# An encoder layer on one core: output weights loaded into the query and key buffers, first feed-forward columns placed inside the output projection

## The chip, the cores and the metric

The kernel runs on one core of a Trainium2 chip. A core has five engines that run side by side, each working through its own list of instructions in order: PE (TensorE, matrix products), ACT (ScalarE), DVE (VectorE), POOL (GpSimd) and SP (SyncE, which here only issues DMA transfers). An instruction that has to wait holds up everything behind it on its engine. The metric is the device time of one execution in microseconds (us); lower is better.

## The reference

One encoder layer on x of 2048 tokens by 1024 channels, all float32. It normalises, projects, mixes by two head groups side by side (dilated attention and a gated MLP), projects the joined halves out, adds, and ends with a squared-ReLU feed-forward part of width 4096.

```python
def hybrid_layer(x, g_pre_mix, w_in, sgu_ln_g, sgu_ln_b, sgu_w, sgu_b, w_out, g_post_mix,
                 g_pre_ffn, w_ff1, w_ff2, g_post_ffn, rel_bias):
    h = rms_norm(x, g_pre_mix)
    z = h @ w_in
    q, k, v, zu, zv = jnp.split(...)
    attn = dilated_attention(q, k, v, rel_bias).reshape(B, S, D_ATTN)
    sgu = spatial_gating(jax.nn.gelu(zu), jax.nn.gelu(zv), sgu_ln_g, sgu_ln_b, sgu_w, sgu_b)
    mix = jnp.concatenate([attn, sgu], axis=-1) @ w_out
    x = x + rms_norm(mix, g_post_mix)
    h = rms_norm(x, g_pre_ffn)
    f = jnp.square(jax.nn.relu(h @ w_ff1)) @ w_ff2
    return x + rms_norm(f, g_post_ffn)
```

## The kernel before, in words

Every float32 product is made of three matmuls: each operand is split into a rounded high part and a remainder (`wh` and `wl`, `mh` and `ml`, `hh` and `hl`, `fh` and `fl`), ACT writing the high part and DVE the remainder, and `mm3` (lines 84 to 86) multiplies low by high, high by low, and high by high. A weight piece of 128 rows by 512 columns is loaded by `piece` into a raw buffer (tile `wraw`) and split into one of eight pairs in the pool `weights`.

The program has three stages.

- **Stage 1** projects x into queries, keys, values and the gated MLP's second half.
- **Stage 2** runs the attention, 8 heads of 12 groups, as a pipeline of 112 steps. The generator `gate` holds PE work that does not depend on attention: the gated MLP's first half, and then, per tile of 128 tokens, the half of the output projection that the gated MLP feeds (PSUM tile `f2`, shown as `f` in the trace), written to DRAM as `part`. `filler` runs pieces of it between the parts of a step, up to a share that `plan` computes; `PRE` and `POST` are the nanoseconds of it that are kept for before the first step and after the last. The order on PE and ACT in stage 2 is fixed as it is written (`in_order`); on the other engines, and in stage 3, a scheduler sets it. In the last tile of `gate`, before the change, `c.wo` is loaded: the eight pieces of `w_out` that belong to attention. They take the buffers of the eight pieces that this tile is using.
- **Stage 3** first does the attention half of the output projection, tile by tile, 16 tiles of 128 tokens. For a tile, `operand` loads the attention output (`fa`) and the reciprocal denominators (`fr`, one row spread over 64 partitions), multiplies them on POOL and splits the product; 24 matmuls into `mo` follow; DVE adds `part` (tile `r`). `post` normalises and adds x (tile `xt`), and writes the result to DRAM as `x1d`. For the first eight tiles, `prep` normalises again (in place, in `r`) and turns the tile by eight transposes (`tp`) into `hh` and `hl`, which the feed-forward part reads. Each of the two norms takes a pass of ACT (`jk`) and two small POOL instructions (`rs`, lines 90 and 91). Then, in two halves of 1024 tokens and eight groups of 512 hidden columns, `ff1` (192 matmuls into `f`) and `ff2` (192 into `g`) run.

Buffers in stage 3 before: three for `r`, two for `xt`, three each for `fa`, `fr`, `mh`, `ml`, five for `fh` and `fl`; six PSUM banks shared by `mo`, `f` and `g`. The core of the loop:

```python
            ahead, behind = 2, 1
            ...
                if i + ahead < 16:
                    ops.append(operand(i + ahead))
                if i + 1 < 16:
                    rx.append(rest(i + 1))
                (mh, ml), (r, xt) = ops.pop(0), rx.pop(0)
                ...
                if len(old) == behind:
                    prep(*old.pop(0))
```

## Time and profile before

| what | value |
|---|---|
| time, median of 3 runs | 2503.76 us (2500.02 to 2510.98) |
| profiled execution: its time | 2515.86 us |
| profiled execution: its span | 2514.0 us |
| busy shares of the span | PE 95%, weight loads 80%, DVE 42%, ACT 37%, POOL 19% |
| stage 2 (409 to 949 us), PE busy | 488.4 of 540 us |
| projection in stage 3 (949 to 1095.5 us), PE busy | 110.1 of 146.5 us |
| the rest of stage 3 (1095.5 us to the end), PE busy | 1403.2 of 1418.5 us |

The span is the time between the first and the last record of the profiled execution; 1.86 us of its time lie around it. Matmuls overlap in the trace (each is shown some 0.4 us long and one starts every 0.23 us), so PE's busy time is not its work: waits are read from the gaps, work from the distance of starts.

### The profile page before, as it was taken

To read this page: it belongs to the slowest core of one execution; us is meant where nothing else is said; L and a number is where in the kernel's file an instruction comes from. 1 tells how busy PE (TensorE), PEld (TensorE's weight loads), DVE (VectorE), ACT (ScalarE), POOL (GpSimd) and SP (SyncE) were. 2 spreads that over 40 slices of the span, in tenths; PEclk is the share of its full clock that TensorE was granted. 3 is DMA by queue.
4 is the path that set the end of the run, shared out by engine and by line. 5 is a ranking of instruction groups with operands and counts; after the bars stand their busy time and mean duration, and the time that the engine had idled before them with its cause. 6 is when DMAs were issued, how large, how long until landed. Compare 5 with 4: busy or idle time off the path is not lost.

```text
span 2514.0 us, 31489 instructions
## 1 busy us (share of the span) xinstructions
PE 2390.3 (95%) x11591; PEld 2000.0 (80%) x11591; DVE 1063.1 (42%) x2246; ACT 934.9 (37%) x2053; POOL 471.2 (19%) x521
## 2 busy tenths in 40 slices
PE   7999999988899996799999999999999999999998
PEld 6787888878788885678888888888788888888887
DVE  5433523566766644551322322333722333233226
ACT  4424322366766673433221221123533122212213
POOL 4103103533222222420100110011211001001101
PEclk9999999989999998899999999999999999999999
DMA  7646365878777567761111111111611121111113
GB/s 269 215 138 201 130 189 159 203 175 195 202 175 173 142 153 204 231 232 59 51 47 38 56 47 49 51 51 59 201 59 51 34 67 46 48 42 51 51 43 125
DMA packets 222077, 296.13 MB, mean 118 GB/s; under 512 B 37089, under 2 KB 128740, under 8 KB 218852
## 3 DMA queue, kind: packets, MB, share of 16 engines
q1 hardware_dynamic: 214724, 273.15, 37.4%
q10 hardware_dynamic: 4640, 16.79, 1.7%
q0 software_dynamic: 2560, 4.20, 1.2%
q8 instruction: 91, 1.49, 0.2%
q14 instruction: 62, 0.51, 0.1%
HBM read 216.04 MB, written 82.74 MB: 119 GB/s over the span
## 4 chain that ended last, share of the span: by engine, by line
PE 75%; DMA 12%; DVE 4%; ACT 3%; issue 1%; POOL 1%; SPq 1%; DVEq 0%; ACTq 0%; POOLq 0%
PE f L84 10%; PE f L85 10%; PE f L86 10%; PE g L86 8%; PE g L84 8%; PE g L85 8%; PE mm L84 4%; PE mm L86 4%; PE mm L85 4%; DMA v<-vd 2%; DMA r<-part 2%; PE t L588 2%; PE o L617 1%; PE o L616 1%; PE s L508 1%
## 5 line engine op out<-in xcount | busy, mean ns | idle before, releaser
L85 PE MATMUL f<-hh,wl 128*128 128x512 f32 x1024 | 399.4, 390 | 2.2 <-DVE wl L57 2.2
L86 PE MATMUL f<-hh,wh 128*128 128x512 f32 x1024 | 399.4, 390 | 0.0
L84 PE MATMUL g<-wl,fh 128*128 128x512 f32 x1024 | 399.4, 390 | 0.0
L84 PE MATMUL f<-hl,wh 128*128 128x512 f32 x1024 | 399.2, 390 | 0.0
L86 PE MATMUL g<-wh,fh 128*128 128x512 f32 x1024 | 398.9, 390 | 0.0
L85 PE MATMUL g<-wh,fl 128*128 128x512 f32 x1024 | 398.8, 390 | 0.0
L979 POOL TENSOR_TENSOR sq<-sq 128x512 f32<-128x512 f32 x128 | 131.9, 1051 | 1161.2 <-ACT sq L978 1161.2
L56 ACT ACTIVATE wh<-wraw,gain 128x512 fp32r<-128x512 f32 x200 | 143.3, 724 | 505.8 <-PE g L86 423.3
L57 DVE SCALAR_TENSOR_TENSOR wl<-wraw,gain,wh 128x512 fp32r<-128x512 f32 x200 | 158.0, 797 | 268.5 <-ACT wh L56 265.6
L60 DVE TENSOR_TENSOR fl<-sq,fh 128x512 fp32r<-128x512 f32 x128 | 99.3, 776 | 394.9 <-ACT fh L59 385.9
L85 PEld LDWEIGHTS f<-hh,wl 128*128 128x128 f32 x1024 | 192.6, 188 | 42.6 <-DVE wl L57 2.6
L84 PEld LDWEIGHTS f<-hl,wh 128*128 128x128 f32 x1024 | 192.7, 188 | 40.0
L86 PEld LDWEIGHTS f<-hh,wh 128*128 128x128 f32 x1024 | 192.6, 188 | 39.9
L86 PEld LDWEIGHTS g<-wh,fh 128*128 128x128 f32 x1024 | 192.3, 188 | 39.8
L85 PEld LDWEIGHTS g<-wh,fl 128*128 128x128 f32 x1024 | 192.3, 188 | 39.6
L84 PEld LDWEIGHTS g<-wl,fh 128*128 128x128 f32 x1024 | 192.3, 188 | 39.6
L1006 DVE TENSOR_TENSOR acc<-g,acc 128x512 f32<-128x512 f32 x192 | 127.2, 688 | 165.1 <-PE g L86 165.1
L978 ACT ACTIVATE sq<-f 128x512 f32<-128x512 f32 x128 | 74.8, 597 | 290.5 <-PE f L86 283.3
L577 ACT ACTIVATE p<-p,m 128x256 f32<-128x256 f32 (+2 forms) x384 | 173.8, 458 | 23.7 <-DVE m L549 23.7
L60 DVE TENSOR_TENSOR wl<-wraw,wh 128x512 fp32r<-128x512 f32 x144 | 100.5, 698 | 175.1 <-ACT wh L59 173.8
L59 ACT CAST wh<-wraw 128x512 fp32r<-128x512 f32 x144 | 89.5, 622 | 186.1 <-PE f L86 172.6
L525 DVE CUSTOM_DVE_ANT_0 p<-s,bias 128x256 f32<-128x256 f32 (+2 forms) x384 | 121.1, 356 | 44.2 <-PE s L509 30.5
(156 smaller groups left out, 4170.7 us busy)
## 6 DMA issues: line engine op xcount, KB each, us to landing
wraw<-in_w_ff_dram SPq DMA_DIRECT2D x256, 256.0 KB, 2.7
wraw<-in_w_in_dram SPq DMA_DIRECT2D x72, 256.0 KB, 3.0
xt<-in_x_dram SPq DMA_DIRECT2D x32, 512.0 KB, 5.6
v<-vd SPq DMA_DIRECT2D x40, 256.0 KB, 6.3
v<-vd SPq DMA_DIRECT2D x8, 1088.0 KB, 7.9
hd<-ht ACTq DMA_DIRECT2D x16, 512.0 KB, 5.1
vd<-vt SPq DMA_DIRECT2D x16, 512.0 KB, 3.1
qd<-e SPq DMA_DIRECT2D x32, 256.0 KB, 2.8
```

The source lines that it names most:

```text
L56: nc.scalar.activation(hi, src, AF.Copy, scale=scale)
L57: nc.vector.scalar_tensor_tensor(lo, src, scale, f32(hi), ALU.mult, ALU.subtract)
L59: nc.scalar.copy(hi, src)
L60: nc.vector.tensor_tensor(lo, src, f32(hi), ALU.subtract)
L84: nc.tensor.matmul(out, lhsT=lh, rhs=rl, start=start, stop=False)
L85: nc.tensor.matmul(out, lhsT=ll, rhs=rh, start=False, stop=False)
L86: nc.tensor.matmul(out, lhsT=lh, rhs=rh, start=False, stop=stop)
L525: nc.vector.tensor_tensor_reduce(po, so, bo, -1.0, 1e38, ALU.add, ALU.min, o.nm[:, br, cc:cc + 1])
L577: nc.scalar.activation(p[:, at + lo:at + hi], p[:, at + lo:at + hi], AF.Exp, bias=o.m[:, br, cc:cc + 1], scale=-1.0, accum_out=o.dn[:, br, ...
L978: nc.scalar.activation(sq, b, AF.Relu)
L979: nc.gpsimd.tensor_tensor(sq, sq, sq, ALU.mult)
L1006: nc.vector.tensor_tensor(av, b, av, ALU.add)
```

## The change

What it does, part by part:

- `c.wo` is no longer loaded in the last tile of `gate`. `attn_piece` loads one piece in each of the steps 96 to 103, after the last scores, into the buffers of queries and keys (`qk_tiles`), which a context of their own (`c.qctx`) now keeps open until the projection is done. ACT's cast and DVE's subtraction of each piece stand in those steps.
- `POST` goes from 4000 to 14000 ns.
- Stage 3 loads `fr` ahead of `fa`, two tiles ahead of the multiplication's tile (`load_attn`), with two buffers each in place of three; `operand` only multiplies and splits, one tile ahead. `part` is loaded two tiles ahead, with four `r` buffers in place of three; three `xt` buffers in place of two.
- The second norm (`normed`) writes into `xt`, no longer in place into `r`; a tile is turned two tiles after its projection, no longer one.
- The first eight `w_ff1` pieces (`ws0`) are loaded in iterations 1 to 4, no longer in the last. Of the first group's 192 `f` matmuls, 96 (`ff1_unit`, columns 0 to 255 of the group) are placed between the `mo` matmuls of tiles 6 to 12; the other 96 come after the loop. `load2(0)` is called before them.
- `fh` and `fl` get two buffers in each of two pools; `gpost` and `gmix` share one buffer; `y` and `xp` move to another pool.

```diff
@@ stage 1 and 2
-        c.qk = c.fctx.enter_context(tc.tile_pool(name="s2q", bufs=2, side="right"))
+        c.qk = c.qctx.enter_context(tc.tile_pool(name="s2q", bufs=2, side="right"))
...
+        c.wo = []
+
+        def attn_piece(k):
+
+            if k % 4 == 0:
+                c.spare = qk_tiles(c)
+            t = c.spare[k % 4 // 2][:, 1024 * (k % 2):1024 * (k % 2) + 1024]
+            raw = fload(nc, c, a["w_out"][0][(k % 4) * P:(k % 4 + 1) * P, (k // 4) * 512:(k // 4 + 1) * 512]
+                        .rearrange("p (k t) -> p k t", k=4))
+            split_sbuf(nc, raw.rearrange("p k t -> p (k t)"), t[:, 0:512], t[:, 512:])
+            c.wo.append((t[:, 0:512], t[:, 512:]))
...
-                        if i == 15:
-                            c.wo.append(out_piece(k * P, n))
...
-        PRE, POST = 8 * 1000.0, 4 * 1000.0
+        PRE, POST = 8 * 1000.0, 14 * 1000.0
...
+            if sa >= NH * NG and len(c.wo) < 8:
+                attn_piece(len(c.wo))
@@ stage 3
-        def normed(x1):
+        def normed(x1, out):
             rs = meansq(x1)
-            nc.scalar.activation(x1, x1, AF.Copy, scale=rs)
+            nc.scalar.activation(out, x1, AF.Copy, scale=rs)
...
+        def ff1_unit(h, ws, c0, es, fs, pool):
+
+            hh, hl = h
+            bs = [pm.tile([P, 512], F32, name=f"f{m}", tag="mm3") for m in range(2 * len(es))]
+            for kc in range(8):
+                wh, wl = ws[kc]
+                for m, b in enumerate(bs):
+                    k, e = divmod(m, len(es))
+                    cs = slice(c0 + k * P, c0 + (k + 1) * P)
+                    ts = slice(es[e] * 512, (es[e] + 1) * 512)
+                    mm3(nc, b, wh[:, cs], wl[:, cs], hh[:, kc, ts], hl[:, kc, ts], kc == 0, kc == 7)
+                yield
...
-            om = octx.enter_context(tc.tile_pool(name="s3m", bufs=3, side="right"))
-            orp = octx.enter_context(tc.tile_pool(name="s3r", bufs=3))
+            om = octx.enter_context(tc.tile_pool(name="s3m", bufs=2, side="right"))
+            orp = octx.enter_context(tc.tile_pool(name="s3r", bufs=4, side="right"))
...
+            parts, xs = [load_part(0), load_part(1)], [load_x(0)]
+            loads = [load_attn(0), load_attn(1)]
+            ops = [operand(*loads.pop(0))]
+            old, ws0, fs0, fs1 = [], [], [], []
+            early = {6: 3, 7: 3, 8: 2, 9: 1, 10: 3, 11: 3, 12: 3}
             for i in range(16):
...
+                (mh, ml), r, xt = ops.pop(0), parts.pop(0), xs.pop(0)
                 if i + 1 < 16:
-                    rx.append(rest(i + 1))
-                (mh, ml), (r, xt) = ops.pop(0), rx.pop(0)
+                    ops.append(operand(*loads.pop(0)))
+                if i + 2 < 16:
+                    loads.append(load_attn(i + 2))
+                if i in (6, 10):
+                    unit = ff1_unit(h, ws0, 0, (i // 10,), fs0, fpa)
                 for n in range(2):
...
                     nc.vector.tensor_tensor(r[:, ns], b, r[:, ns], ALU.add)
+                    for _ in range((early.get(i, 0) + 1 - n) // 2):
+                        next(unit, None)
+                if len(old) == 2 or i == 9:
+                    turned(*old.pop(0)[1:])
+                if i + 2 < 16:
+                    parts.append(load_part(i + 2))
+                if i + 1 < 16:
+                    xs.append(load_x(i + 1))
+                if 1 <= i < 5:
+                    ws0 += [piece(nc, c, w1[kc * P:(kc + 1) * P, 0:512], scale=c.gffn[:, kc:kc + 1])
+                            for kc in range(2 * i - 2, 2 * i)]
+                if 0 < i <= 8:
+                    normed(*old[-1][:2])
+                post(i, r, xt)
                 if i < 8:
-                    old.append((r, h[0], h[1], i))
-            for x in late:
-                post(*x)
-
+                    old.append((r, xt, h[0], h[1], i))
+        c.qctx.close()
+        v0 = load2(0)
+        fpb = ctx.enter_context(tc.tile_pool(name="s3g", bufs=2))
+        for _ in ff1_unit(h, ws0, 256, (0, 1), fs1, fpb):
+            pass
```

How the built programs differ at three places. First SP's list of transfers where the projection's first loads stand, in the program of before (`rd` holds the denominators, `wraw<-in_w_out` are `c.wo`'s pieces, `r` is `part`'s tile):

```order
L570 DMA rd<-d 128x16
L711 DMA part<-ot 128x512
L66 DMA wraw<-in_w_out_dram 128x512 x2
L895 DMA fr<-rd 64x4x128
L66 DMA wraw<-in_w_out_dram 128x512
L895 DMA fr<-rd 64x4x128
L905 DMA r<-part 128x1024
L895 DMA fr<-rd 64x4x128
```

The same place in the program of the change:

```order
L66 DMA wraw<-in_w_ff_dram 128x512 x2
L721 DMA part<-ot 128x512
L66 DMA wraw<-in_w_ff_dram 128x512 x3
L942 DMA r<-part 128x1024 x2
L927 DMA fr<-rd 64x4x128 x2
L928 DMA fa<-od 128x4x128
L927 DMA fr<-rd 64x4x128 x2
L928 DMA fa<-od 128x4x128
```

The `c.wo` pieces are gone from here; eleven loads of feed-forward weights stand between the last ones of `part<-ot`, the last three of them behind the very last, and the first `r`, `fr` and `fa` follow behind those.

Second POOL's list from the first products `fa` on, before. `rs_10033` is the first norm's factor of tile 0, `rs_10084` that of tile 1, `rs_10093` the second norm's of tile 0, the one that the transposes need:

```order
L898 TENSOR_TENSOR fa<-fa,fr 128x512 x4
L90 TENSOR_SCALAR rs_10033<-ms_10031 128x1
L91 TENSOR_TENSOR rs_10033<-rs_10033,mhalf 128x1
L898 TENSOR_TENSOR fa<-fa,fr 128x512
L90 TENSOR_SCALAR rs_10084<-ms_10082 128x1
L91 TENSOR_TENSOR rs_10084<-rs_10084,mhalf 128x1
L898 TENSOR_TENSOR fa<-fa,fr 128x512
L90 TENSOR_SCALAR rs_10093<-ms_10091 128x1
L91 TENSOR_TENSOR rs_10093<-rs_10093,mhalf 128x1
```

And with the change, where `rs_10015` and `rs_10078` are the two factors of tile 0 and `rs_10085` the first of tile 1:

```order
L935 TENSOR_TENSOR fa<-fa,fr 128x512 x4
L90 TENSOR_SCALAR rs_10015<-ms_10013 128x1
L91 TENSOR_TENSOR rs_10015<-rs_10015,mhalf 128x1
L935 TENSOR_TENSOR fa<-fa,fr 128x512
L90 TENSOR_SCALAR rs_10078<-ms_10076 128x1
L91 TENSOR_TENSOR rs_10078<-rs_10078,mhalf 128x1
L90 TENSOR_SCALAR rs_10085<-ms_10083 128x1
L91 TENSOR_TENSOR rs_10085<-rs_10085,mhalf 128x1
L935 TENSOR_TENSOR fa<-fa,fr 128x512
```

The second factor of tile 0 now stands behind five products, before it stood behind six.

Third PE's list in the first half of tile 6, with the change: `tp` turns tile 3, and the first moved `f` matmuls, which read `hh` and `hl` of tiles 0 to 3, stand two `mo` matmuls behind it. Before, only `mo` rows stood around the transposes.

```order
L84 MATMUL mo<-ks,mh 128x512
L876 MATMUL tp_10381<-ident,xt_10145 128x128 x4
L876 MATMUL tp_10388<-ident,xt_10145 128x128 x4
L85 MATMUL mo<-ks,ml 128x512
L86 MATMUL mo<-ks,mh 128x512
L84 MATMUL f_10439<-hl_9937,wh 128x512
L85 MATMUL f_10439<-hh_9936,wl 128x512
L86 MATMUL f_10439<-hh_9936,wh 128x512
L84 MATMUL f_10440<-hl_9937,wh 128x512
```

The first transposes stand behind 72 `mo` matmuls (three tiles) with the change and behind 76 before, and later ones follow every 24 to 32 in both. Between the last attention product `o` of stage 2 and the first `mo` stand 69 `f` matmuls with the change, 21 before.

## Rows read from the trace of the kernel before

**Rows 1.** Stretches: busy us (and instructions) of each engine, granted clock, DMA share, GB/s.

```profile
409.00:949.00 540.00, 488.42 (x3162) 433.45 (x3160) 332.35 (x1197) 336.85 (x1053) 187.13 (x187) 0.94 0.73 181
949.00:961.30 12.30, 0.15 (x1) 0.00 (x0) 3.57 (x8) 3.61 (x7) 2.07 (x2) 0.61 0.82 223
961.30:1095.50 134.20, 109.90 (x447) 87.50 (x448) 74.73 (x88) 53.08 (x86) 48.11 (x59) 0.88 0.77 230
1095.50:1143.10 47.60, 45.44 (x193) 37.14 (x192) 22.52 (x29) 21.59 (x34) 9.86 (x13) 0.96 0.46 156
...
1080.00:1090.00 10.00, 10.00 (x44) 8.03 (x44) 6.18 (x7) 1.15 (x2) 0.79 (x2) 1.00 0.94 342
1200.00:1700.00 500.00, 500.00 (x2207) 414.17 (x2206) 160.55 (x232) 117.92 (x188) 49.47 (x48) 1.00 0.16 49
```

**Rows 2.** PE's waits from 949 to 1143 us: total us, times, longest.

```profile
PE tp L870 <- ACT r L863: 24.2, 7, 9.7
PE mo L84 <- ACT mh L59: 12.2, 1, 12.2
PE f L85 <- DVE wl L57: 2.2, 1, 2.2
```

**Rows 3.** PE in order of time: start, us, operation, [idle before, releaser].

```profile
948.75 0.40 PE L86 MATMUL f<-wh,xh 128*128 128x512 f32 x1
961.31 0.79 PE L84 MATMUL mo<-wl,mh 128*128 128x512 f32 x1 [12.17 <-ACT mh L59]
...
965.19 0.49 PE L86 MATMUL mo<-wh,mh 128*128 128x512 f32 x1
...
970.20 0.40 PE L86 MATMUL mo<-wh,mh 128*128 128x512 f32 x1
...
980.04 0.40 PE L86 MATMUL mo<-wh,mh 128*128 128x512 f32 x1
...
1000.39 1.10 PE L870 MATMUL tp<-ident,r 128*128 128x128 f32 x8
1001.25 0.48 PE L86 MATMUL mo<-wh,mh 128*128 128x512 f32 x1
```

**Rows 4.** Other engines' waits in the projection's loop, 961.3 to 1095.5 us.

```profile
POOL fa L898 <- DMA fa<-od: 23.2, 5, 6.6
...
ACT r L863 <- DMA x1d<-r: 10.3, 4, 3.5
```

**Rows 5.** The chain that ended last, 936 to 1000 us: start, us, what.

```profile
980.58 6.84 DMA fr<-rd
```

**Rows 6.** Transfers issued from 949 to 1096 us: count, KB each, median us to landing.

```profile
DMA packets 23044, 33.84 MB, mean 230 GB/s; under 512 B 1744, under 2 KB 15824, under 8 KB 23036
...
fr<-rd SPq DMA_DIRECT2D x29, 128.0 KB, 10.3
fa<-od SPq DMA_DIRECT2D x13, 256.0 KB, 8.3
```

**Rows 7.** All engines in order of time, at the projection's first tile.

```profile
954.68 0.62 SPq L895 DMA_DIRECT2D fr<-rd  x1
...
956.71 0.33 SPq L905 DMA_DIRECT2D r<-part  x1
...
959.36 1.25 POOL L898 TENSOR_TENSOR fa<-fa,fr 128x512 f32<-128x512 f32 x1 [6.14 <-DMA fr<-rd]
...
961.69 0.58 ACT L710 COPY ot<-f 128x512 f32<-128x512 f32 x1
```

**Rows 8.** Costliest groups, the page's part 5: busy us, mean ns.

```profile
L56 ACT ACTIVATE wh<-wraw,gain 128x512 fp32r<-128x512 f32 x200 | 143.3, 724 | 505.8 <-PE g L86 423.3
L57 DVE SCALAR_TENSOR_TENSOR wl<-wraw,gain,wh 128x512 fp32r<-128x512 f32 x200 | 158.0, 797 | 268.5 <-ACT wh L56 265.6
```

**Rows 9.** Waits in stage 2, 409 to 949 us: total us, times, longest.

```profile
PE o L616 <- DMA v<-vd: 16.7, 14, 3.3
...
ACT wh L59 <- DMA wraw<-in_w_out_dram: 6.3, 3, 4.0
```

More of the change, by code (lines that the diff above doesn't have):

```diff
@@ L879, in stage3, with load2, load_attn @@
         h = new_h()
-        w1s = []
-        with ExitStack() as octx:
-            op = octx.enter_context(tc.tile_pool(name="s3o", bufs=1, side="right"))
-            om = octx.enter_context(tc.tile_pool(name="s3m", bufs=3, side="right"))
-            orp = octx.enter_context(tc.tile_pool(name="s3r", bufs=3))
-            gmix = bcast_row(nc, op, a["g_post_mix"][0:1], D, "gmix")
-            def operand(i):
+        fpa = ctx.enter_context(tc.tile_pool(name="s3f", bufs=2))
+        def ff1_unit(h, ws, c0, es, fs, pool):
[9 more added lines that the diff above has]
+                yield
+            for k in range(2):
+                if len(fs) == k:
+                    fs.append(tuple(pool.tile([P, 1024], F32R, name=x, tag=x) for x in ("fh", "fl")))
+                fh, fl = fs[k]
+                for e in range(len(es)):
+                    ts = slice(es[e] * 512, (es[e] + 1) * 512)
+                    sq = wk.tile([P, 512], F32, name="sq", tag="sq")
+                    nc.scalar.activation(sq, bs[k * len(es) + e], AF.Relu)
+                    nc.gpsimd.tensor_tensor(sq, sq, sq, ALU.mult)
+                    split_sbuf(nc, sq, fh[:, ts], fl[:, ts])
+        def load2(g):
+            return [[piece(nc, c, w2[(4 * g + k) * P:(4 * g + k + 1) * P, n * 512:(n + 1) * 512]) for k in range(4)]
+                    for n in range(2)]
+        with ExitStack() as octx:
+            om = octx.enter_context(tc.tile_pool(name="s3m", bufs=2, side="right"))
+            orp = octx.enter_context(tc.tile_pool(name="s3r", bufs=4, side="right"))
+            gmix = bcast_row(nc, cst, a["g_post_mix"][0:1], D, "gmix", "gain")
+            def load_attn(i):
                 sl = slice(i * P, (i + 1) * P)
@@ L1013, in done @@
                 def done(i, bs):
-                    x1 = wk.tile([P, D], F32, name="xf", tag="xt3")
+                    x1 = wk.tile([P, D], F32, name="xf", tag="xt3", bufs=3)
                     rows = slice(i * P, (i + 1) * P)
@@ L1019, in done @@
                     ms = sm.tile([P, 2], F32, name="ms4", tag="ms4")
-                    y = wk.tile([P, D], F32, name="y", tag="y", bufs=1)
+                    y = ap_.tile([P, D], F32, name="y", tag="y", bufs=1)
                     for n, b in enumerate(bs):
@@ L1046, in stage3 @@
                 for g in range(NG):
-                    v = load2(g)
-                    fs = ff1(h, ws)
+                    v, fs = (v0, fs0 + fs1) if half == g == 0 else (load2(g), ff1(h, ws))
                     last = g == NG - 1
```

78 lines of the change are left out of this document (22 added, 56 removed).

## The prediction

> **What bounds the kernel now.** I read the stretches first. From 1200 to 1700 us PE starts 2207 matmuls in 500 us without a gap, one every 0.2266 us at full clock [rows 1]: the feed-forward part is PE's own work, and nothing in the change makes it less. Stage 2 has PE busy 488.4 of 540 us [rows 1], its gaps scattered over many small waits, the largest kind 16.7 us in 14 pieces [rows 9]. The stretch between the two is different: from 949.0 (the last `f2` matmul starts at 948.75 [rows 3]) to the first `g` at 1143.1 us pass 12.3 + 134.2 + 47.6 = 194.1 us [rows 1].
>
> How much of that is work? `mo` starts come every 0.2343 us (42 steps from 970.20 to 980.04 [rows 3]), so 384 take 90.0. Eight transposes hold PE for 0.86 us (1000.39 to 1001.25 [rows 3]), 64 take 6.9. 192 `f` at 0.2266 take 43.5. Sum 140.4. PE's waits are 24.2 + 12.2 + 2.2 = 38.6 [rows 2]. The rest, 194.1 - 140.4 - 38.6 = 15.1 us, is the lower clock after waits: the granted clock is 0.88 in the loop and 0.96 behind it [rows 1]; after the first wait, eight steps take 3.88 us (961.31 to 965.19 [rows 3]) where 1.87 would do. So some 54 us in this stretch are not work, and they are all that the change can reach.
>
> What stands behind the waits: the 12.2 us at the start end with ACT's `mh` cast, behind POOL's product and the `fr` transfer [rows 2, 7]. The 24.2 us are PE standing in front of the transposes until ACT has written the second norm. Behind that stand POOL, which reaches the norm's factor only after products that wait for `fa` (23.2 us) [rows 4] and `fr` (once 6.84 us on the chain [rows 5]), and ACT itself, 10.3 us, because the norm is written in place and the `x1d` transfer must have read `r` first [rows 4].
>
> **The change part by part.**
>
> *The moved `f` matmuls.* 96 of 192 go between the `mo` of tiles 6 to 12: 96 x 0.2266 = 21.8 us of PE work. They add no work; they are worth something only as far as they fill waits. I count the work as 140.4 as before.
>
> *The waits for the transposes (24.2 us and their clock).* The transposes stand at nearly the same place in PE's list (behind 72 `mo`, before 76), so turning a tile "two later" is not by itself what helps. What helps is upstream. The norm goes to `xt`: the 10.3 us of waiting for `x1d` [rows 4] have no cause left. Tile 0's second factor stands behind five products on POOL, before behind six. `fr` and `fa` are issued ahead of the `xt` load that waited for tile 0's `post` on SP. I followed tile 0 by hand: the fifth product needs `fa`'s second buffer free, which tile 2's split gives once the first tile's `mo` are through; with some 5 us to land and 1.25 for the product, the norm is there 18 us after the first `mo`, and PE reaches the transposes after 3 x 24 x 0.2343 + 2.0 = 18.9. Now it is there after 29.7 (first `mo` at 961.31, transposes at 980.04 + 0.9 + the wait of 9.7 [rows 2, 3], about 991). So that one goes. But it is close, and two buffers in place of three for `fa` and `fr` make the next loads later: tile 5's `fa` stands on SP behind an `r` load that needs the first tile's norm, so I expect some 3 us at tile 1, 1 us each at tiles 3 to 5, and 2 us in front of the first moved `f`, which need tile 3's `hh` and `hl` two `mo` after its transposes. Together 8 us, clock included. The bounds are 0 and all that is lost now, 24.2 plus the 13.1 of clock that is not the start's.
>
> *The start (12.2 us).* `POST` leaves 48 more matmuls, 11 us, behind the last attention product, so denominators and attention outputs are written before `f2` ends. But the loads do not start then. In SP's list eleven `w_ff` loads stand before the first `r`, `fr` and `fa`. With four raw buffers, the eleventh needs the seventh weight piece split; its pair of buffers is one of the eight that `f2`'s last tile is using, so the seventh is freed by nearly the last matmul. From the end of `f2`: the `ot` copy 0.58 [rows 7], the fifth to seventh casts partly behind it, two whole ones of 0.72, then the subtraction 0.80 [rows 8]: 2.8, with the fifth's remainder 3.2. Then SP issues one raw load and two `r` at 0.33, two `fr` at 0.62 [rows 7] and `fa`: to 5.8. Before, 4.06 us passed from the end of the last `fr` issue to POOL's start (955.30 to 959.36 [rows 7]), then 1.95 to the first `mo` at 961.31. That gives 5.8 + 4.06 + 1.95 = 11.8 us. The wait stays, under another name: I take 12.0, with 2.0 of clock. Below, 4 us less if the weight chain runs ahead; above, 16 us, if `fr` lands as in the loop (10.3 us [rows 6]).
>
> *The wait at the first `f` (2.2 us)* goes: its weights are split before the loop.
>
> *DMA.* From 949 to 1096 us 33.84 MB move at 230 GB/s [rows 6]; the change takes some 2.5 MB of weights and `part` out and puts 1.2 MB of `fa` and `fr` in, about 33 MB. The loop as I sum it ends 12 + 2 + 90.0 + 6.9 + 21.8 + 8 = 140.7 us after `f2`, so 33 MB have 137 us: 240 GB/s. One stretch of ten us reached 342 at a share of 0.94 [rows 1]. The trace thus leaves room, and I charge nothing; at 230 it would be 7 us more. The Trainium skill says against it ("DMA: Bandwidth & Descriptors", section "Issuing engines are not separate DMA queues") that transfers issued from several engines run on the same 16 DMA engines and interleave, so that issuing earlier adds no capacity. By that rule alone, with the loop's mean rate taken as the capacity, the sum is 7 us worse; this trace's 342 GB/s says that the mean is not the capacity.
>
> *Stage 2.* PE's work stays; 10 us of filler leave the steps. Where PE waits for others anyway (a tenth of the time: 51.6 of 540 us [rows 1]) a step does not get shorter: about 1 us. The eight casts of `attn_piece` stand in ACT's fixed order and wait for their raw loads there; behind each stand the exponentials and the `th` casts that PE needs. The eight `w_out` casts already in stage 2 waited 6.3 us in 3 places, at most 4.0 [rows 9]; ACT is busy 336.9 of 540 us [rows 1] and so has slack: I take 1 us for PE. Together 2, bounds 0 and 8 x 4.0 = 32.
>
> *The rest.* The buffers of `fh` and `fl` fall from five to four, but `ff1` writes the next group's only after 96 matmuls (21.8 us), when the last group's readers on PE are done: 0, and without that cover one evacuation per group. `gpost` waits for `gmix`'s last use at the loop's end, seven groups of `ff1` and `ff2` before it is read: 0. `w_ff1`'s first pieces leave the end of the loop, which I have counted.
>
> **Sum.** 140.4 + 12.0 + 2.0 + 8 = 162.4 in place of 194.1: 31.7 less; stage 2 gives back 2: 29.7 less. The profiled execution took 2515.86, so 2486.2, which is 0.9882 of it; its time stands 12 us above the median of the runs, and 0.9882 of 2503.76 is 2474.
>
> **The rivals.**
> *DMA holds the loop* at its present 230 GB/s: 33 MB take 143.5 us from 3.5 us on, the loop ends 6 to 7 us later, 2481. For it: `fr` already lands after 10.3 us and `fa` after 8.3 [rows 6]. Against: the stretches at 342. The skill's rule above is this rival's.
> *The start is covered:* if the eleven `w_ff` loads do not hold SP, the filler hides the start, 12 + 2 us more gain: 2460. For it: everything that `fa` and `fr` need is written by then. Against: the order on SP.
> *The transposes' waits stay:* PE reaches them at the same place, and POOL's factor still stands behind products that wait for transfers. Then 24.2 + 13.1 in place of 8, gain below 1 us: 2503, no change. Half of it is 2489.
> *Slower:* the eight casts in stage 2 each hold ACT, and PE behind it. At 4.0 us each [rows 9] it is 32, and the gain is gone (2504); at 6 us each 48, 2520. It decides from about 4 us each. For it: the order on ACT is fixed and three raw buffers serve both the pieces and the filler. Against: `w_out` casts wait 6.3 us in all now.
>
> **How the numbers follow.** Forecast 0.57 (2466 to 2480 by itself), DMA 0.14, covered start 0.12, waits stay or half stay 0.11, stage 2 stalls 0.06. Two times are told apart here from about 0.5%, 12.5 us (below 2491 is faster). The forecast, DMA and the covered start are faster, and a part of the half-stayed waits: 0.85. No change: 0.09. Slower: 0.06. The range from 2457 (covered start, and a little less in the loop) to 2491 (half of the waits stay) leaves out both tails.
>
> **What would show it.** Right: the first `mo` some 12 us after the last `f2`, waiting for `mh` behind `fr` and SP behind the `wraw` loads; PE's waits for the transposes below 10 us; the loop some 141 us from `f2`'s end with 480 matmuls in it; 96 `f` (21.8 us) from there to the first `g`; stage 2 within 3 us of now. Wrong: `mo` starting right after `f2`; ACT waiting for `w_out` pieces in steps 96 to 103 by more than 10 us with PE gaps behind; a DMA share near 0.95 through the loop with PE waiting for `mh`.

## The result, and the profile after

The changed kernel takes 2538.33 us (median of 4 runs, 2537.27 to 2547.69), the kernel before beside it 2505.47 us: the ratio is 1.0139, 95% interval 1.0106 to 1.0173. It is 1.4% slower, where 1.2% faster was forecast. One of q13's five executions (3515.97 us) and one of q14's ten (3370.47 us) ran at a mean granted clock of 0.63 and 0.65, and no time or ratio below counts them. The profiled execution of the changed kernel took 2547.69 us, its span is 2545.9.

The stretches of the changed kernel, which answer to [rows 1] (same columns): stage 2, then from 949.0, 0.8 us after the end of `f2`, to the first `mo`, from there to the last `mo`, and from there to the first `g`.

```profile
409.00:948.20 539.20, 489.70 (x3156) 431.39 (x3155) 339.54 (x1205) 341.50 (x1061) 186.25 (x188) 0.94 0.73 185
949.00:969.10 20.10, 0.00 (x0) 0.00 (x0) 3.13 (x6) 3.34 (x6) 1.26 (x1) 0.59 0.71 203
969.10:1149.70 180.60, 133.03 (x543) 105.75 (x544) 78.61 (x97) 56.06 (x93) 41.94 (x65) 0.88 0.54 165
1149.70:1171.80 22.10, 22.10 (x99) 18.23 (x99) 8.56 (x11) 10.89 (x18) 3.92 (x8) 1.00 0.70 238
```

From the end of the last `f2` (948.2) to the first `g` (1171.8) pass 223.6 us, where 194.1 passed before and 162.4 were forecast. PE's waits in this stretch, which answer to [rows 2]:

```profile
PE mo L84 <- ACT mh L59: 24.6, 2, 20.8
PE tp L876 <- ACT xt L869: 18.6, 5, 7.0
PE f L84 <- DVE hl L76: 12.4, 2, 11.1
PE tp L876 <- DVE hl L76: 9.9, 2, 8.8
PE mo L85 <- DVE ml L60: 2.8, 2, 1.9
```

Their sum is 68.3 us; before it was 38.6. The work is 140.4 us as the prediction counts it, so 223.6 - 140.4 - 68.3 = 14.9 us are left for the lower clock, as 15.1 were before. The stretch is 29.5 us longer and the waits 29.7: all that was lost in it is waiting. Behind the first `g` the two kernels take the same time within 4 us (1374.1 and 1370.7 us to the end of the span).

In the loop, ACT no longer waits for `x1d` in front of the second norm (10.3 us before [rows 4]); it waits there for POOL's factor, 24.9 us in place of 18.2:

```profile
ACT xt L869 <- POOL rs L91: 24.9, 8, 6.0
```

So the waits for the transposes did not fall: 18.6 + 9.9 = 28.5 us, where 24.2 passed before.

The start, all engines in order of time (start, us, operation, wait before it): SP is at its `w_ff` loads until 954.3; the first `fr` is issued at 955.58, the first product starts at 967.15, the first `mo` at 969.12.

```profile
950.18 4.15 SPq L66 DMA_DIRECT2D wraw<-in_w_ff_dram  x3
954.74 0.80 SPq L942 DMA_DIRECT2D r<-part  x2
955.58 1.30 SPq L927 DMA_DIRECT2D fr<-rd  x2
956.92 0.60 SPq L928 DMA_DIRECT2D fa<-od  x1
...
967.15 1.26 POOL L935 TENSOR_TENSOR fa<-fa,fr 128x512 f32<-128x512 f32 x1 [24.50 <-DMA fr<-rd]
...
969.12 0.80 PE L84 MATMUL mo<-qs,mh 128*128 128x512 f32 x1 [20.76 <-ACT mh L59]
```

The loop around tiles 6 to 8, by the chain of work that ended last (start, us, what): one product, the next issue on SP, one transfer, the next product, and nothing beside it, a tile every 10 to 11 us.

```profile
1017.81 1.26 POOL fa L935
...
1019.38 0.29 SPq L927
...
1019.77 8.39 DMA fa<-od
...
1028.29 1.29 POOL fa L935
...
1029.89 0.29 SPq L927
...
1030.27 8.72 DMA fa<-od
...
1039.22 1.29 POOL fa L935
```

SP's own rows there tell why: `fr` of a later tile (line 927) stands ahead of `fa` of the next one (line 928), waits until a product has given its buffer free, and holds the `fa` load behind it, whose own buffer is free already (for the load at 1019.77 since 1013.1, when DVE had split tile 5).

```profile
1019.10 0.58 SPq L927 DMA_DIRECT2D fr<-rd  x1
1019.77 0.56 SPq L928 DMA_DIRECT2D fa<-od  x1
1020.38 0.67 SPq L927 DMA_DIRECT2D fr<-rd  x1
...
1029.60 0.58 SPq L927 DMA_DIRECT2D fr<-rd  x1
1030.27 1.29 SPq L928 DMA_DIRECT2D fa<-od  x1
1031.61 0.58 SPq L927 DMA_DIRECT2D fr<-rd  x1
```

In the built program the order on SP is fr(i+2), fa(i+1) from `fa` of tile 5 on. Before, `fa` of tile 8 was issued ahead of `part` of tile 4 (994.15 and 1002.37 us) and `fr` of tile 8 just behind it (from 1004.18). There, the attention loads ran about four tiles ahead of the rest.

That order is what holds the loads of tiles 6 to 10. Of the 47.5 us that PE waits in the loop, 27.6 come after 1062 us, where the products, but for the last, are 13.9 to 17.4 us apart, and there three things take turns on SP. `fa` of tiles 11 and 13 waits until DVE's split of the tile two before (`ml`) has given its buffer free:

```profile
1064.33 0.54 SPq L942 DMA_DIRECT2D r<-part  x1
1068.59 0.69 DVE L60 TENSOR_TENSOR ml<-fa,mh 128x512 fp32r<-128x512 f32 x1 [1.49 <-ACT mh L59]
1069.31 0.38 SPq L928 DMA_DIRECT2D fa<-od  x1
...
1092.36 1.03 SPq L947 DMA_DIRECT2D xt<-in_x_dram  x2
1094.88 0.68 DVE L60 TENSOR_TENSOR ml<-fa,mh 128x512 fp32r<-128x512 f32 x1
1095.59 1.66 SPq L928 DMA_DIRECT2D fa<-od  x1
```

`fa` of tiles 12 and 14 goes out behind `fr` of a later tile as above (`fr` at 1077.39 and 1108.46), and `fa` of tile 15 stands behind an `r` load that waits for `x1d` (until 1122.25). So the loop's loss has more than the one cause.

### The profile page after: what moved, and what is told of

Read it like the earlier page. It is cut to its first block, busy times and chain, and to the rows that moved or that the text cites. A ratio compares the mean times of both kernels' runs of the same rounds, so it can differ in the third digit from the quotient of the medians.

```text
span 2545.9 us, 31494 instructions
## 1 busy us (share of the span) xinstructions
PE 2393.3 (94%) x11591; PEld 1998.8 (79%) x11591; DVE 1061.1 (42%) x2246; ACT 933.7 (37%) x2053; POOL 457.5 (18%) x521
## 4 chain that ended last, share of the span: by engine, by line
PE 61%; DMA 10%; DVE 4%; ACT 3%; POOL 2%; issue 1%; SPq 1%; ACTq 0%; POOLq 0%; DVEq 0%
PE f L84 10%; PE f L85 10%; PE f L86 10%; PE g L86 8%; PE g L84 8%; PE g L85 8%; DMA fa<-od 3%; DMA v<-vd 2%; PE t L588 2%; PE o L617 1%; PE o L616 1%; PE s L508 1%; ACT p L577 1%; PE s L509 1%; POOL fa L935 1%
## 5 line engine op out<-in xcount | busy, mean ns | idle before, releaser
L84 PE MATMUL f<-hl,wh 128*128 128x512 f32 x1024 | 399.3, 390 | 12.4 <-DVE hl L76 12.4
L85 PEld LDWEIGHTS g<-wh,fl 128*128 128x128 f32 x1024 | 192.5, 188 | 39.8
L577 ACT ACTIVATE p<-p,m 128x256 f32<-128x256 f32 (+2 forms) x384 | 174.0, 459 | 18.9 <-DVE m L549 18.9
L60 DVE TENSOR_TENSOR wl<-wraw,wh 128x512 fp32r<-128x512 f32 x136 | 94.0, 691 | 167.9 <-ACT wh L59 166.6
```

The costliest lines, as they stand in the source:

```text
L60: nc.vector.tensor_tensor(lo, src, f32(hi), ALU.subtract)
L84: nc.tensor.matmul(out, lhsT=lh, rhs=rl, start=start, stop=False)
L85: nc.tensor.matmul(out, lhsT=ll, rhs=rh, start=False, stop=False)
L577: nc.scalar.activation(p[:, at + lo:at + hi], p[:, at + lo:at + hi], AF.Exp, bias=o.m[:, br, cc:cc + 1], scale=-1.0, accum_out=o.dn[:, br, ...
```

## The experiments

Each kernel was timed beside the kernel before. In the table, "start" is from the last `f2` to the first `mo`, "loop" from the first to the last `mo`, "behind" from there to the first `g`, and "stretch" their sum, all in us from the profiled execution. "Products" is the mean distance of POOL's products from the second to the last. The time of one kernel moves by up to 17 us from run to run (the kernel before: 2500.29 to 2517.43 in 23 runs), and in the profiles the last `f2` moves as far as that from kernel to kernel, so causes are read from the stretch. It comes from one profiled execution of each kernel, and how far it moves between executions is not known; the changed kernel and q9, whose lists on SP are the same from tile 5 on, agree in the loop to 0.1 us.

| kernel | start | loop | behind | stretch | products | time, us | ratio (95%) |
|---|---|---|---|---|---|---|---|
| before | 12.6 | 134.2 | 47.8 | 194.6 | 7.9 | | |
| changed | 21.2 | 180.6 | 22.0 | 223.8 | 11.3 | 2538.3 | 1.0139 (1.0106 to 1.0173) |
| q1 order on SP | 20.6 | 163.1 | 22.0 | 205.7 | 10.0 | 2532.7 | 1.0097 (1.0076 to 1.0118) |
| q2 no interleaving | 20.4 | 153.2 | 43.8 | 217.4 | 10.3 | 2543.2 | 1.0129 (1.0101 to 1.0158) |
| q3 before, two buffers | 11.9 | 149.3 | 47.4 | 208.6 | 9.8 | 2523.2 | 1.0059 (1.0036 to 1.0081) |
| q4 `w_ff` loads back | 17.2 | 182.6 | 22.0 | 221.8 | 11.5 | 2541.6 | 1.0138 (1.0117 to 1.0159) |
| q5 other memory | 8.4 | 188.8 | 22.0 | 219.2 | 11.8 | 2540.0 | 1.0126 (1.0111 to 1.0142) |
| q6 q5 and q1 | 8.7 | 171.9 | 22.0 | 202.6 | 10.5 | 2525.7 | 1.0063 (1.0040 to 1.0087) |
| q7 before, moved | 25.4 | 152.6 | 47.5 | 225.5 | 9.1 | 2527.0 | 1.0079 (1.0049 to 1.0108) |
| q8 three buffers | 20.1 | 166.4 | 22.0 | 208.5 | 9.7 | 2527.3 | 1.0086 (1.0058 to 1.0115) |
| q9 `r` one ahead | 19.5 | 180.6 | 22.0 | 222.1 | 11.3 | 2542.1 | 1.0142 (1.0123 to 1.0160) |
| q10 q6 and q9 | 8.9 | 169.0 | 22.0 | 200.0 | 10.3 | 2522.7 | 1.0064 (1.0045 to 1.0084) |
| q11 q10, three buffers | 9.7 | 169.2 | 22.0 | 201.0 | 10.0 | 2528.6 | 1.0089 (1.0072 to 1.0106) |
| q12 q10, half of `fr` | 7.8 | 165.6 | 22.0 | 195.4 | 10.0 | 2520.7 | 1.0053 (1.0034 to 1.0071) |
| q13 q10, further ahead | | | | | | 2529.8 | 1.0085 (1.0068 to 1.0102) |
| q14 q13, POST 4 | 19.4 | 165.3 | 22.0 | 206.7 | 10.0 | 2515.1 | 1.0026 (1.0015 to 1.0037) |
| q15 changed, POST 4 | 22.7 | 193.0 | 22.0 | 237.8 | 12.2 | 2552.1 | 1.0173 (1.0152 to 1.0195) |
| q16 before, POST 14 | 6.3 | 143.3 | 48.8 | 198.4 | 8.5 | 2520.6 | 1.0046 (1.0031 to 1.0062) |
| q17 before, norm apart | 13.0 | 125.8 | 56.0 | 194.9 | 8.0 | 2503.6 | 0.9990 (0.9973 to 1.0006) |
| q18 q17, four `r`, `xt` | 12.5 | 137.8 | 51.7 | 201.9 | 9.3 | 2513.9 | 1.0019 (1.0003 to 1.0035) |

The changed kernel's loop is 46.4 us longer than the one before, of which 21.8 are the moved `f`: 24.6 us were lost there, and 8.6 at the start.

### q1 and q8: the loads that stand behind each other on SP

q1 ties each attention load to the one written before it, so that SP issues them tile by tile; the tie sets an order and no wait.

```diff
+                for x in nc.cur_bb.bb.instructions[at:]:
+                    if "DMA" in type(x).__name__:
+                        if chain:
+                            tc.add_manual_dep(x, chain[-1].name, ..., reason="order")
+                        chain.append(x)
```

> The changed kernel, with SP's list of the attention loads made fr(i), fa(i), fr(i+1), fa(i+1); in the changed kernel fr(i+2) stands ahead of fa(i+1). Nothing else is asked for. Theory Q (order on SP: fa(i+1), whose buffer is free, stands behind fr(i+2), which waits for the product of tile i; load, product and next load run one after the other, 10.7 us per tile): POOL's products come every 8 to 9 us, the stretch from the first to the last mo falls from 180 to about 140 us, POOL's wait for fa from 74 us to below 30; about 2500 us. Theory D (the transfers themselves are at their limit): products still 10.7 us apart, 2538. Theory I (the interleaved f and the later turning hold ACT, DVE and POOL): within 5 us of 2538.

The loop falls by 17.5 us and the stretch by 18.1, so the order on SP is one cause. Theory Q had a loop of 140, and it is 163: a part of it. POOL's waits for `fa` did not fall below 30 us as it said, they are 92.5 (74.0 before the tie, with 32.2 for `fr` that are now gone). The times alone do not part the two kernels: their intervals overlap. Theory I, which expected no change, falls as the only cause.

q8 gives `fa` and `fr` the third buffer back, at the cost of one of `r`.

```diff
-            orp = octx.enter_context(tc.tile_pool(name="s3r", bufs=4, side="right"))
+            orp = octx.enter_context(tc.tile_pool(name="s3r", bufs=3, side="right"))
-                fa = om.tile([P, 4, P], F32, name="fa", tag="fa")
+                fa = om.tile([P, 4, P], F32, name="fa", tag="fa", bufs=3)
```

> The changed kernel, with three buffers for fa and fr in place of two, and three for r in place of four to make room; nothing else is edited. Theory Q: fr(i+2) has a free buffer when it comes to its turn on SP, fa(i+1) behind it goes at once, the products no longer come every 10.7 us: the loop falls from 180 to 160 us or less, the time to about 2520, or more where the missing r buffer makes SP wait. Theory D (the DMA engines are full): no change, 2538. The start stays at 20 to 21 us by either.

The loop falls by 14.2 us, to 166.4, short of the 160 of theory Q, with the start moved by 1.1 only. The time is 2527.3, so theory D, which expected 2538, falls. `mh` and `ml` keep their two buffers here.

### q3: two buffers in the kernel before

```diff
-            om = octx.enter_context(tc.tile_pool(name="s3m", bufs=3, side="right"))
+            om = octx.enter_context(tc.tile_pool(name="s3m", bufs=2, side="right"))
```

> The kernel before, with two buffers in place of three for fa, fr, mh and ml, and nothing else changed. Theory Q: the third buffer is what let the next loads go; without it load, product and split come closer to one chain, but fr and fa of one tile still stand side by side on SP: 2510 to 2530, PE's waits in the loop up by 5 to 25 us. Theory D and theory I: 2505, no change.

The loop grows by 15.1 us, the time by 0.6%. PE's waits, with the transposes' as they were (25.4 for 24.2) and a new one for `ml`:

```profile
PE tp L870 <- ACT r L863: 25.4, 8, 10.6
PE mo L84 <- ACT mh L59: 11.9, 2, 11.5
PE mo L85 <- DVE ml L60: 11.5, 3, 4.8
```

So with two buffers and nothing else of the change, the loop loses 15.1 us, where the changed kernel's loses 24.6. The prediction's 6 us for it (3 at tile 1, 1 each at tiles 3 to 5) were too few by 9. The edit takes the third buffer from `fa`, `fr`, `mh` and `ml` together; which of them costs what is not parted.

### q2: the interleaving

```diff
-            early = {6: 3, 7: 3, 8: 2, 9: 1, 10: 3, 11: 3, 12: 3}
+            early = {}
```

(with all 192 `f` behind the loop).

> The changed kernel with no f matmul between the mo: all 192 f stand behind the loop. Theory Q: the products stay some 10.7 us apart, so the loop is still 165 to 175 us, and the 96 f (21.8 us) that then stand behind it come on top: 2535 to 2560. Theory I: the loop falls by the 21.8 us of f and by the waits at the f as well, to about 135 us, and the time to about 2515. Theory D: as Q.

The loop is 27.4 us shorter, 21.8 of which are the `f` themselves, and 21.7 come back behind it. Theory Q had 165 to 175 for this loop and theory I 135; it is 153.2, between them. The stretch is 6.4 us shorter, and the time is not told apart from the changed kernel's. So the interleaving caused little of the loss, if any, and filled no waits that show: where `f` stands between the `mo`, PE waits in front of it instead (12.4 us for `hl` in the changed kernel), and with none there the transposes wait 31.7.

### q4, q5 and q7: the start

q4 puts the loads of the first `w_ff1` pieces behind the first attention loads.

> The changed kernel, with the loads of the first w_ff1 pieces put behind the first two fr and fa on SP (in the changed kernel eleven stand ahead of them). Theory H (the start is held by those loads, on SP and in the DMA queue): the first mo comes 9 to 12 us after the last f2, not 20.8, and the time falls by 8 to 12 us, to about 2528. If it were the writing of the denominators and attention outputs that ends last, the first mo stays at 20 us and the time at 2538. The loop behind it keeps its 10.7 us per tile in either case.

The start falls by 4.0 us only, and the time not at all, so theory H accounts for less than half of the 8.6 us that the start lost. In the built program lies another reason. Before, `fa`, `fr`, `mh` and `ml` are in the memory of queries and keys, which is free when the last scores are done: SP issues the first `fa` at 940.88, 8 us ahead of the last `f2`. The change puts the output weights there, and `fa`, `fr`, `mh` and `ml` fall on the addresses of `f2`'s operands `xh` and `xl` and of its result `ot`. q5 moves the first two tiles elsewhere, into the buffers that take `fh` and `fl` later:

```diff
-                fa = om.tile([P, 4, P], F32, name="fa", tag="fa")
-                fr = om.tile([P, 4, P], F32, name="fr", tag="fr")
+                if i < 2:
+                    two = fpa.tile([P, 8, P], F32, name="fafr", tag="fh")
+                    fa, fr = two[:, 0:4, :], two[:, 4:8, :]
```

> The changed kernel, with fa, fr, mh and ml of the first two tiles held in the buffers that later take fh and fl; nothing else is edited. Theory M (memory): with the output weights in the buffers of queries and keys, fa, fr, mh and ml lie where f2's operands and results lie, so their loads wait for the last f2 and for the last transfer of part; in the other place they are free when attention ends. By M the first two fr and fa are issued before f2 ends, the first mo starts 1 to 5 us after the last f2 in place of 21.2, and some 17 us go. Theory H (the w_ff loads on SP and in the DMA queue hold the start; held back by themselves they gave 4 us): the first mo comes at 17 to 21 us. The edit also moves SP's order: fr(i+2) stands ahead of fa(i+1) from tile 8 on, not from tile 5, so by theory Q the loop falls by some 6 to 10 us of the 17.5 that the full order gave. M and Q together: about 2513; H and Q: 2530.

The first `mo`, after an 8.0 us wait in place of 20.8:

```profile
957.47 0.79 PE L84 MATMUL mo<-qs,mhml 128*128 128x512 f32 x1 [8.02 <-ACT mhml L59]
```

The start falls by 12.8 us, to 8.4 (theory M had 1 to 5), and the first `fr` is issued at 945.22, ahead of the last `f2`. The edit moved the order on SP too: the `w_ff` loads now stand behind these first loads, from 952.98 on, and that alone gave 4.0 us in q4. If the two simply add, some 8.8 us are the memory's. But the loop takes 8.2 us back, and the time does not move by what can be told. q7 is the mirror, in the kernel before:

```diff
+            gap = pad.tile([P, 7168], F32, name="gap", tag="gap")
             om = octx.enter_context(tc.tile_pool(name="s3m", bufs=3, side="right"))
```

> The kernel before, with 28 KB of each partition left unused behind the gains, so that fa, fr, mh and ml lie where f2's operands lie; nothing else is edited. Theory M: fa of the first tiles, issued 6 to 8 us ahead of the last f2 in the kernel before, now waits for it; the first mo comes 18 to 21 us after the last f2, not 12.6, and the time is 6 to 10 us longer, 2512 to 2517. If the place of the buffers does not matter: 2505 and 12.6.

```profile
953.08 0.79 PE L84 MATMUL mo<-wl,mh 128*128 128x512 f32 x1 [25.02 <-ACT mh L59]
```

The start doubles, to 25.4 us, with no other line edited, and the loop grows by 18.4. The last `f2` came at 927.7 us, 21 earlier, so the time grew by 0.8% only; the last attention product stands 4.8 us ahead of it in both kernels, so the start did not grow by `f2`'s ending early. But the order on SP moved with the memory: the first `fa` now stands behind the first `r` loads and the last `part`. So place and order together cost the start, and no run moves the place alone.

### q6, q9, q10, q11: both together, and the loads of r

q6 is q5 with the tie of q1. q9 and q10 load `r` one tile ahead in place of two, in the changed kernel and in q6:

```diff
-            parts, xs = [load_part(0), load_part(1)], [load_x(0)]
+            parts, xs = [load_part(0)], [load_x(0)]
...
-                if i + 2 < 16:
-                    parts.append(load_part(i + 2))
+                if i + 1 < 16:
+                    parts.append(load_part(i + 1))
```

> The kernel of q5 with SP's attention loads in the order of q1 through the whole loop. M and Q: the start of q5 (1 to 5 us) and the loop of q1 (163 us from the first to the last mo, 180 in the changed kernel) add up: about 2503. If the two work on the same time (the loop waits for the same transfers, however early the first), the loop grows by what the start gives, and the time stays near 2520 to 2530.

> The changed kernel, with the load of r (rows of part) written one tile ahead in place of two; four buffers as before; nothing else is edited. Theory S (a load of r waits on SP for the x1d transfer of the tile whose buffer it takes, with the attention loads behind it; 51.5 us of such waits in the profile of q6): one ahead, the buffer is that of a tile earlier by one, long stored, and the loop falls by 5 to 20 us. Theory Q alone (fr(i+2) ahead of fa(i+1) is the lock; that order is left here): within 5 us of the changed kernel, 2538.

> The kernel of q6 with the loads of r one tile ahead in place of two. Theory S: SP's waits for x1d fall from 51.5 us to below 10, POOL's waits for fa from 47 us to below 30, the loop from 172 to 150 to 160 us, the time from 2526 to 2505 to 2515. Theory D (the transfers of fa, 8 to 12 us each, bound the loop, whatever stands ahead of them on SP): within 4 us of 2526.

q6 has both gains in the stretch, 202.6 us, 21.2 less than the changed kernel; against q1 its start falls by 11.9 us, of which the loop takes 8.8 back, and its time is the 2526 of the case in which the two work on the same time. q9 changes nothing (SP still waits 31.0 us for `x1d` in front of `r`), but it is no test of theory S in most of the loop: from tile 5 on the scheduler issued `r`, `fr` and `fa` in the order of the changed kernel. In q10 that wait falls from 57.6 to 33.6 us, not below 10, other loads wait in its place, and the loop falls by 2.9. Here too the order of q6 comes back, from `r` of tile 8 on. So theory S is not borne out, and not ruled out; the time, 2522.7, is what theory D named for this run. First q6, then q10, SP's waits from 945 to 1140:

```profile
SPq L960 <- DMA x1d<-r: 57.6, 11, 9.2
```

```profile
SPq L960 <- DMA x1d<-r: 33.6, 8, 6.4
SPq L935 <- DVE ml L60: 23.9, 6, 7.9
```

In q10 PE waits 39.8 us in all, as in the kernel before (38.6). With order, memory and `r` changed, the waits are back where they were before the change, and nothing is gained: the stretch is still 5.4 us longer than before. q11 adds the third buffers to q10, with three of `r`:

> The kernel of q10 with three buffers for fa and fr and three for r. Theory B (two buffers are too few for transfers of 9 us: the kernel before lost 14 us in this stretch with two): the loop falls by another 5 to 14 us, to about 2500, at or a little below the kernel before, since start and loop then have all that it has. Against it: with three buffers of r one ahead, r waits for x1d again, as in q6: 2515 to 2526.

It gained nothing (201.0 for 200.0); SP waits 49.1 us for `x1d` again, as the case against it said.

### q12: is it the DMA engines?

Half of the `fr` transfers from tile 3 on are left out; the tile takes the denominators of the tile before, so the products of these seven tiles are other numbers.

> The kernel of q10 with the transfers of fr left out for every other tile from tile 3 on, which takes the denominators of the tile before (so half of the products are other numbers). Theory D (the DMA engines' time, much of it in short packets of fr and fa, bounds the loop): 7 of 16 tiles lose 256 KB of such packets, at 4 to 5 us each: the loop falls by 15 to 30 us against q10. If it is the order and the buffers alone: below 8 us.

The loop falls by 3.4 us and the stretch by 4.6, below the 8 that were named for order and buffers alone. So the DMA engines' time is not what bounds q10's loop. In the changed kernel, where this was not tried, their share in the loop is 0.54, with 0.77 before.

### q13 to q16: looking further ahead, and POST

q13 lets loads and products run further ahead, with four sets of buffers up to tile 7; q14 is q13 with `POST` 4.

```diff
-                if i < 2:
+                if i < 8 and i % 4 < 2:
...
+                last = min(i + 2, 7) if i < 7 else min(i + 1, 15)
```

> The kernel of q10, with the attention loads three to four tiles ahead and the products two ahead up to tile 7 (one behind it): tiles 4 and 5 use the buffers of fh and fl again, as tiles 0 and 1 do, so four sets of buffers serve the first eight tiles. Theory L (lookahead): what makes the loop wait is that a load is issued only one product ahead, and lands 9 us later; four sets cover it, POOL's waits for fa fall from 73 to below 35 us, PE's waits in the loop from 31 to below 15, the stretch from the last f2 to the first g from 200 to 175 to 188, the time to 2498 to 2510. Theory D (the DMA engines' time): more loads at once share the same engines, each lands later, and the stretch stays at 195 to 202: 2518 to 2524.

> The kernel of q13 with POST 4 in place of 14. Theory P (with the start free, filler behind the last product covers the landing of the first denominators, and costs about as much ahead of it): first mo 12 to 15 us after the last f2 in place of about 9, last f2 4 to 8 us earlier, time within 5 us of q13. If the moved filler costs stage 2 more than it covers: 5 to 10 us below q13.

Of q13 only the time is used: 2530, outside what either theory named, so theory L is not borne out, and its waits are not known. q14 is the best of this row of kernels, 15 us below q13, more than either case had, and 0.3% above the kernel before. Its start is 19.4 us, not 12 to 15, since its first loads wait for the last attention outputs (SP issues `fr` at 946.80).

`POST` alone, in the changed kernel and in the kernel before:

```diff
-        PRE, POST = 8 * 1000.0, 14 * 1000.0
+        PRE, POST = 8 * 1000.0, 4 * 1000.0
```

> The changed kernel with POST 4 in place of 14, nothing else. Theory M (the first attention loads wait for the last f2 because of the memory they lie in): the filler behind the last product covers nothing, the first mo stays 20 to 22 us after the last f2, the last f2 comes 3 to 8 us earlier, and the time falls by that: 2530 to 2535. If the filler did cover the landing of the denominators: 2540 to 2548.

> The kernel before with POST 14 in place of 4, nothing else. Here the first fa lie in the buffers of queries and keys, free in time. Theory P: the first mo comes 4 to 8 us after the last f2 in place of 12.6, the last f2 3 to 5 us later, and the time falls by 0 to 5 us: 2502 to 2507. If the moved filler costs stage 2 more: 2510 to 2515.

Both times lie above all that was expected. In q15 the `w_ff` loads that stood ahead of the start move into the loop between the attention loads, ACT waits 19.2 us for them (4.0 in the changed kernel), and the loop grows by 12.4. In q16 the start falls from 12.6 to 6.3 us, as theory P said, and the loop takes 9.1 back. What `POST` costs stage 2 shows over all profiles: with 14, the last `f2` starts at 949.6 us in the mean of 12 kernels (943.1 to 958.3), with 4 at 943.6 in the mean of 6 (939.8 to 948.8; q7 not counted). The two ranges overlap, so the 6 us between the means are an estimate.

### q17 and q18: the norm by itself

The kernel before with the second norm written to `xt` (three buffers, in memory that lay unused), and then with four buffers of `r` and `xt`.

```diff
-            nc.scalar.activation(x1, x1, AF.Copy, scale=rs)
+            nc.scalar.activation(out, x1, AF.Copy, scale=rs)
```

> The kernel before, with the second norm written to xt in place of over r, and three buffers for xt (in memory that lay unused in the loop); nothing else is edited. If the norm over r is what holds ACT (10.3 us in front of the norm, and the transposes 24.2 us behind it): ACT's wait for x1d is gone, PE's waits for the transposes fall to 10 to 18 us, and the time by 4 to 12 us, to 2496 to 2504. If POOL's factor, which stands behind the products and their transfers, is what comes last: ACT waits for POOL in place of x1d, the transposes keep 20 to 25 us, and the time is within 4 us of 2508.

> The kernel of q17 with four buffers for r and xt. Theory S (r's loads wait on SP for x1d, 14.9 us in the kernel before, and hold the attention loads behind them): another 3 to 8 us less than q17. If the lead of the attention loads is enough here: within 3 us of q17.

q17's loop is 8.4 us shorter, and the wait for `x1d` in front of the norm is gone. In its place ACT waits 19.0 us for POOL's factor, and the transposes' waits fall from 24.2 to 18.9, so both cases had a part. But its first `f` are reached before their weights are split, and 8.2 us come back behind the loop; the time is the same. PE's waits in q17:

```profile
PE tp L870 <- ACT xt L863: 18.9, 5, 6.9
PE mo L84 <- ACT mh L59: 12.6, 1, 12.6
PE f L85 <- DVE wl L57: 7.5, 1, 7.5
PE f L84 <- ACT wh L56: 2.5, 1, 2.5
```

q18 lost the loop's gain again, against both of its cases. q17 with the early `w_ff1` pieces of the change, which would be there before the last two rows, was not tried.

## Why the prediction was wrong, step by step

The stretch was forecast at 162.4 us and took 223.6. The error of 61.2 us is 8.9 at the start, 51.9 in the loop and 0.4 behind it.

- **What bounds the kernel:** right. Of the 31.9 us by which the spans differ, 29.5 lie in the stretch that the prediction chose, and these are all PE's waits.
- **The loop's waits (forecast 8 us, clock included): the step that failed.** It said that the norm's wait for `x1d` has "no cause left", and that two buffers in place of three cost "some 3 us at tile 1, 1 us each at tiles 3 to 5". The first half is right: ACT no longer waits for `x1d`, and q17 gives 8.4 us in the loop for it. The second half followed SP's list by hand as far as tile 5, and just there the order turns: from then on fr(i+2) stands ahead of fa(i+1). The measured waits in the loop are 47.5 us; in front of the first moved `f`, priced at 2, they are 12.4. Of the 24.6 us that the loop lost, the order is worth 17.5 (q1) and two buffers by themselves 15.1 (q3); these overlap, as a third buffer for `fa` and `fr` gives back 14.2 (q8) and not the sum. What was priced at the first tiles is paid through the whole loop.
- **The waits for the transposes, expected below 10 us, measured 28.5:** they are the largest part of the 47.5. The rival by which they stay (0.11) had the reason, POOL's factor behind products that wait for transfers: ACT waits 24.9 us for it. It did not have the products coming 11.3 us apart in place of 7.9.
- **The start (forecast 11.8, measured 20.9):** the mechanism on SP was right, `w_ff` loads first and then `r`, `fr`, `fa`. The term that was mis-sized is the landing: 4.06 us were taken from the row of before [rows 7], 10.3 passed (956.88 to 967.15), and the issue came 2.9 us later than forecast. In the row of before `fa` had been loaded long since and only `fr` was under way; here `r`, `fr` and `fa` of two tiles go at once (that this is why they land later is argued, no run shows it). That the buffers had moved into `f2`'s memory was not seen. No attention load was issued before `f2` ended, as they were before the change and again in q5, so the covered start, a rival at 0.12, was not open.
- **The moved `f`:** 22.0 us behind the loop as counted. As filler they are worth nothing that can be told (q2).
- **DMA, charged at nothing:** nothing in the runs speaks against it, and q12 bears it out in q10's loop. The rule that the prediction weighed (the Trainium skill, "DMA: Bandwidth & Descriptors", section "Issuing engines are not separate DMA queues") is about transfers issued from several engines; that issuing earlier adds no capacity was drawn from it. It does not decide here: the share fell from 0.77 to 0.54 while the loop grew.
- **Stage 2 (forecast 2):** the casts of `attn_piece` wait 9.0 us in 4 places, at most 4.4, and the row of PE busy is as before. By the means above some 6 us for `POST`, where 1 was taken for it; in the two profiles compared here the last `f2` comes 0.8 us earlier than before.
- **The slower rival** had the right sign and the wrong place: ACT in stage 2. The price of the queue on SP, which is what happened, stood in the text as a remark and not as a rival.

Still open: why the loop takes back most of what an earlier start gives (q5, q16), and what holds q10's products at 10.3 us where the kernel before has 7.9. Three buffers for `fa` and `fr`, one tile less of lead for `r`, half of the `fr` transfers and loads further ahead did not settle it. A third buffer for `mh` and `ml`, which the kernel before has, was given back to no kernel of the change (q13 and q14 have more sets up to tile 7 only).

## What to carry to other kernels

A queue that issues in order is priced over the whole loop: write its list out past the point where buffers are first used again, and ask of each load whose release it waits for and what free load stands behind it. Keeping a buffer in use for longer moves the pools that would have come into its place, so look up whose addresses the next stage's first loads fall on. And a wait removed upstream is worth only as much as the next thing lets it be: q17 gained 8.4 us in the loop and lost 8.2 behind it to weights that were not ready.

## What the runs showed of the hardware

The loads of `fa` and `fr` take some 8 us also where the DMA engines are far from full. In q14, `fr` and `fa` of the first tile are issued from 946.80 to 948.81 and the product starts at 957.24, 8.4 us later. The windows (columns as in [rows 1]) show no engine busy, the DMA share at 0.17 and 0.41, and the granted clock of PE at 0.50, the lower of its two levels, 1.2 GHz:

```profile
947.00:953.00 6.00, 0.00 (x0) 0.00 (x0) 0.00 (x0) 0.00 (x0) 0.00 (x0) 0.50 0.17 31
948.00:957.00 9.00, 0.00 (x0) 0.00 (x0) 0.00 (x0) 0.00 (x0) 0.00 (x0) 0.50 0.41 114
```

So neither the mean rate nor the share tells how long such a load takes. That it helps to issue it still earlier is not shown: q14 issues three to four tiles ahead up to tile 7, and its loop is 3.7 us shorter than q10's.

The Trainium skill ("DMA: Bandwidth & Descriptors", section "Anatomy of one DMA — SWDGE (gpsimd) path") gives 2.0 us and the size over 436 GB/s for a transfer issued from GpSimd, an estimate of 2.6 us for the 256 KB of `fa`; the loads of `fa`, issued from SP, do not agree with it. The issuing engine and the size are not the reason, for the `w_ff` loads of the same size, issued from SP as well, come close to it (kernel before, KB each, median us to landing, over the whole program):

```profile
wraw<-in_w_ff_dram SPq DMA_DIRECT2D x256, 256.0 KB, 2.7
```

Most of these run where the DMA share is 0.16 [rows 1]; four of them inside the loop of before took 8.2 us. `fa` is read in rows of 128 numbers and `w_ff` in rows of 512; whether that makes the 8 us at a low share, no run tests.

The Trainium skill's rule to issue a DMA early and wait for it late (same page, "Rules for kernel authors") is what the loop of before did with its third buffer; q3, without it, is 15.1 us slower in the loop.
